# A written order for the mLSTM row factors, the attention splits and silu(z) in a hybrid decoder layer

## The chip, the cores and the metric

The kernel runs on one core of a Trainium2 chip. The metric is the device time of one launch in microseconds; for the kernel before it is the median of three runs. A fourth launch was taken by the profiler, and all rows below come from that one execution.

## The reference

One decoder layer on a sequence of 256 tokens and a width of 1024, all in float32: a half-step SwiGLU feed-forward block, a mixer, a second half-step feed-forward block, each with an RMS norm whose output is scaled and shifted by a vector made from the condition `c`, and a final RMS norm. The mixer is the part at hand:

```python
proj = h @ w_in                                  # q, k, v of attention, x_m, z
o_a = rmsnorm(attention(q_a, k_a, v_a), attn_norm)
x_conv = silu(causal_depthwise_conv(x_m))
h_m = mlstm(q_m, k_m, v_m, gates)                # num / max(|den|, exp(-m)) per row
h_m = (h_m - mean) * rsqrt(var + EPS) * mlstm_norm
o_m = (h_m + mlstm_skip * x_conv) * silu(z)
return concatenate([o_a, o_m]) @ w_out
```

With 256 tokens the attention has one block, so that it is plain causal attention of eight heads; the mLSTM has four heads of width 128.

## The kernel before

Data lie transposed: 128 features on the partitions, the 256 tokens along the free axis. Every weight is float32 and is split into a high and a low part (`whi` by a ScalarE copy, `wlo` by a VectorE subtraction, in pieces of 128x1024), every activation likewise (`hh`, `hl`; `hilo`, line 342), and a product is three matmuls (`mm3`, line 232): high by high, low by high, high by low. TensorE does little but these. Weights come in chunks of up to 1 MB through SP's DMA queue; a chunk gives two pieces, and five pieces of each kind fit, so a piece can be split as soon as the piece five places ahead of it has been multiplied (`weights`, line 219).

The order of the instructions on each engine is partly written, partly planned. The kernel hands its instructions to a planner, which lays each engine's instructions out by when it takes them to be ready. An instruction issued through `act`, `dve`, `pool` or `pe` while that engine's `on` flag is set is pinned: it stands behind the instruction issued just before it on the same engine in the program, whether or not that one was pinned itself. An unpinned one (the weight splits among them) can be put into any gap ahead of a pinned one that isn't ready. All loads on SP are pinned. The table load that ScalarE needs before a silu is put in after planning.

The stretch that is touched is the end of the mixer (lines 974 to 1011). In the program's order: the last attention pieces and `a_out` (pinned); the rest of the mLSTM sums; the third of four passes over the z columns (`next(g)`, each pass 24 matmuls, whose result goes through `shifted` into `zs`); `m_factors`, which makes one factor per token and head from the row sums (square, max, add, Ln, Exp, three VectorE operations of `newton`, and `spread`, which splits the result into `rows`); `z_silu(0)`, the silu of the first half of z; the fourth z pass; `z_silu(1)`; `m_out_pre` per head; and `hilo` of the attention tiles 1 to 3 into `hh[:, 1..3]` and `hl[:, 1..3]`. The output projection follows: its eight steps k (24 matmuls each) take the attention tiles (k = 0 to 3) and then the mLSTM tiles (k = 4 to 7). Tile 0 has a place of its own (`mix0`), split early. After step k = 2, `m_spread` lays the row factors over 128 partitions by four matmuls on `rows`; then `m_out` makes the mLSTM tiles. TensorE's order is pinned from line 974 to the end of step k = 3; ScalarE's and VectorE's is not pinned from line 981 on, but for the two `z_silu`, which are always pinned. The factor `mlstm_skip` is multiplied into `xc` by four ScalarE copies (line 986), and silu of z by four GpSimd products (line 822).

Of the kernel before, what the change touches and what calls it, by code (L numbers as in the profile page):

```python
# [13 lines left out]
AF = mybir.ActivationFunctionType  # L14
ALU = mybir.AluOpType
# [3 lines left out]
T = 256  # L19
# [4 lines left out]
NH = 4  # L24
# [12 lines left out]
C_SK = 128  # L37
# [23 lines left out]
def layer(ctx: ExitStack, tc: tile.TileContext, i, out: bass.AP):  # L61
# [511 lines left out]
    with tc.tile_pool(name="mix", bufs=1) as mp:  # L573
        mixer(tc, nc, i, mp, locals())
# [13 lines left out]
def mixer(tc, nc, i, mp, L):  # L588
    act, dve, pool, pe, sp = L["act"], L["dve"], L["pool"], L["pe"], L["sp"]
    nm, bank, t256, as32, dma = L["nm"], L["bank"], L["t256"], L["as32"], L["dma"]  # L590
    weights, part, mm3, hilo = L["weights"], L["part"], L["mm3"], L["hilo"]
    sm, hh, hl, tmp, eps_t = L["sm"], L["hh"], L["hl"], L["tmp"], L["eps_t"]
# [5 lines left out]
    def mt(shape, name, dt=F32, tag=None, bufs=1):  # L598
        return mp.tile(shape, dt, name=nm(name), tag=tag or name, bufs=bufs)

    def tiles(*done):

        w = weights()
        for g in range(2):
            pb = bank("b")
            for d in range(8):
                mm3(pb[:, 0:W], w, (g * 8 + d) * P, hh[:, d], hl[:, d], start=(d == 0), stop=(d == 7))
            done[g](pb)
            yield

    def shifted(dst):

        def done(pb):
            col = tmp.tile([P, 1], F32, tag="col", name=nm("col"), bufs=3)
            act.activation(col, pb[:, T:T + 1], AF.Copy)
            t = t256("ht", bufs=3)
            dve.tensor_tensor(t, r, pb[:, 0:T], ALU.mult)
            act.activation(dst, t, AF.Identity, bias=col)
        return done
# [42 lines left out]
    xc = mt([P, NH, T], "xc")  # L662
# [37 lines left out]
    def spread(src):  # L700

        act.activation(rows[0:4], src, AF.Copy)
        dve.tensor_tensor(rows[32:36], src, as32(rows[0:4]), ALU.subtract)
# [84 lines left out]
    def m_vars(h):  # L788
        pe.matmul(st["prow"][0:4, T:2 * T], ohc[:, h], st["sq", h], start=False, stop=(h == NH - 1),
                  skip_group_check=True)  # L790

    def m_factors():


        prow, em = st["prow"], st["em"]
        dd = mt([NH, T], "dd", tag="R2")
        act.activation(dd, prow[0:4, 0:T], AF.Square, scale=EPS ** 0.5)
        dve.tensor_tensor(dd, dd, em, ALU.max)
        vv = mt([NH, T], "vv", tag="R3")
        dve.scalar_tensor_tensor(vv, prow[0:4, T:2 * T], 1.0 / P, dd, ALU.mult, ALU.add)  # L800
        rs = mt([NH, T], "rs", tag="R1")
        act.activation(rs, vv, AF.Ln)
        act.activation(rs, rs, AF.Exp, scale=-0.5)
        newton(rs, vv, [NH, T], "r", 0.0)
        spread(rs)
# [4 lines left out]
    def mix(k):  # L810
        return mix0 if k == 0 else (hh[:, k, 0:T], hl[:, k, 0:T])

    zs = mt([P, NH, T], "zs")

    def z_silu(h2):
        z2 = zs[:, 2 * h2:2 * h2 + 2]
        tc.keep_in_program_order(act.activation(z2, z2, AF.Silu))

    def m_out_pre(h):

        dve.scalar_tensor_tensor(cn[:, h], cn[:, h], sm[:, C_MN + h:C_MN + h + 1], zs[:, h], ALU.mult, ALU.mult)
        pool.tensor_tensor(xc[:, h], xc[:, h], zs[:, h], ALU.mult)

    def m_spread():
        st["pb"] = [bank("b") for _ in range(2)]
# [13 lines left out]
    oa = mt([P, 4, T + 3], "oa", tag="A")  # L839
# [142 lines left out]
    m_sums(3)  # L982
    m_vars(1)
    m_vars(2)
    for h in range(NH):
        act.activation(xc[:, h], xc[:, h], AF.Copy, scale=sm[:, C_SK + h:C_SK + h + 1])
    g = tiles(shifted(zs[:, 2]), shifted(zs[:, 3]))
    side(1)
    next(g)
    m_vars(3)  # L990
    m_factors()
    z_silu(0)
    next(g)
    z_silu(1)
    for h in range(NH):
        m_out_pre(h)
    for j in range(1, 4):
        hilo(*mix(j), oa[:, j, 0:T])
    po = [bank(t) for t in ("m", "m", "a", "a")]
    for c in range(4):  # L1000
        w = weights()
# [100 lines left out]
```

## Time and profile before

| what | value |
|---|---|
| median of three runs | 534.91 us (534.86 to 535.97) |
| profiled execution, its own time | 537.05 us |
| its span, first to last instruction | 535.2 us |
| TensorE matmul busy | 517.4 us, 97% |
| VectorE busy | 423.4 us, 79% |
| ScalarE busy | 281.0 us, 53% |
| GpSimd busy | 46.9 us, 9% |
| mean granted TensorE clock | 0.989 |

An engine's busy time is the sum of its recorded instructions; shares are of the span. The granted clock is given as a share of the full one, 1.00 for 2.4 GHz and 0.50 for 1.2 GHz.

### The profile page before, as it was taken

What the parts mean: (1) busy time and instruction counts of PE and PEld (TensorE: products, weight loads), DVE (VectorE), ACT (ScalarE), POOL (GpSimd) and SP (SyncE); (2) the same over time, 40 slices, a digit from 0 to 9 for tenths busy, and PEclk for the clock granted to TensorE, in tenths of its full rate; (3) what the DMA queues carried; (4) which work ended last, traced back from release to release, by engine and by line L of the source; (5) the groups of instructions that cost most, each with busy time, mean ns of one, the idle gap of its engine ahead of it and who ended that gap; (6) DMA issues with size and microseconds to landing.
All of it is one profiled execution on the core that took longest, in us unless ns stands there. A gap on an engine that the chain in (4) does not pass through costs nothing.

```text
span 535.2 us, 9560 instructions
## 1 busy us (share of the span) xinstructions
PE 517.4 (97%) x3804; PEld 485.3 (91%) x3804; DVE 423.4 (79%) x714; ACT 281.0 (53%) x486; POOL 46.9 (9%) x64
## 2 busy tenths in 40 slices
PE   7999999899999999999999989999999999999992
PEld 7899999899988889988987889999999999988881
DVE  7898879999889997898885686989986776655423
ACT  4464436355555544566767554865545455544410
POOL 5000000000001110110000020400000000022220
PEclk9999999899999999999999999999999999999998
DMA  8997977988778998578631024488955455455002
GB/s 311 356 411 298 381 282 294 349 351 325 300 286 329 328 344 303 172 287 319 225 146 59 15 105 141 184 326 293 312 195 186 163 196 193 157 206 188 1 1 78
DMA packets 23951, 125.73 MB, mean 235 GB/s; under 512 B 2657, under 2 KB 2913, under 8 KB 14434
## 3 DMA queue, kind: packets, MB, share of 16 engines
q1 hardware_dynamic: 23618, 124.59, 62.2%
q8 instruction: 30, 0.49, 0.4%
q10 hardware_dynamic: 288, 0.52, 0.3%
q14 instruction: 15, 0.12, 0.1%
HBM read 124.05 MB, written 1.05 MB: 234 GB/s over the span
## 4 chain that ended last, share of the span: by engine, by line
PE 89%; DVE 4%; DMA 3%; issue 2%; ACT 1%; SPq 0%; DVEq 0%; ACTq 0%
PE psa L54 42%; PE psb L54 27%; PE psm L54 21%; DMA ada<-in_ada 2%; DMA x<-in_x 1%; DVE junk L54 1%; DVE wlo L54 1%; ACT whi L54 0%; DVE cn L54 0%; DVE u_out L54 0%; ACT sq L54 0%; DVE nw L54 0%; DVE half L54 0%; ACT zs L54 0%; DVE x L54 0%
## 5 line engine op out<-in xcount | busy, mean ns | idle before, releaser
L54 ACT ACTIVATE whi<-raw 128x1024 fp32r<-128x1024 f32 (+1 forms) x160 | 167.2, 1047 | 137.8 <-PE psa L54 62.4
L54 DVE TENSOR_TENSOR wlo<-raw,whi 128x1024 fp32r<-128x1024 f32 (+1 forms) x160 | 193.3, 1211 | 53.2 <-ACT whi L54 51.8
L54 PE MATMUL psa<-hh,whi 128*128 128x258 f32 (+1 forms) x388 | 110.1, 286 | 0.6 <-DVE gm L54 0.6
L54 PE MATMUL psa<-hh,wlo 128*128 128x258 f32 (+1 forms) x388 | 110.3, 286 | 0.0
L54 PE MATMUL psa<-hl,whi 128*128 128x258 f32 (+1 forms) x388 | 108.8, 285 | 0.0
L54 PE MATMUL psb<-hh,whi 128*128 128x258 f32 (+1 forms) x316 | 91.3, 290 | 2.3 <-ACT hh L54 1.2
L54 DVE SCALAR_TENSOR_TENSOR junk<-ada,c_bc 128x1024 bf16<-128x1024 f32 x72 | 88.1, 1224 | 3.4 <-DMA ada<-in_ada 3.3
L54 PE MATMUL psb<-hh,wlo 128*128 128x258 f32 (+1 forms) x316 | 89.4, 284 | 0.0
L54 PE MATMUL psb<-hl,whi 128*128 128x258 f32 (+1 forms) x316 | 88.9, 283 | 0.0
L54 PEld LDWEIGHTS psa<-hh,whi 128*128 128x128 f32 x388 | 74.4, 192 | 0.8 <-DVE gm L54 0.8
L54 PEld LDWEIGHTS psa<-hh,wlo 128*128 128x128 f32 x388 | 74.4, 192 | 0.1
L54 PEld LDWEIGHTS psa<-hl,whi 128*128 128x128 f32 x388 | 73.9, 192 | 0.0
L54 PEld LDWEIGHTS psb<-hh,whi 128*128 128x128 f32 x316 | 59.8, 189 | 5.3 <-issue 1.4
L54 PEld LDWEIGHTS psb<-hh,wlo 128*128 128x128 f32 x316 | 59.7, 189 | 0.1
L54 PEld LDWEIGHTS psb<-hl,whi 128*128 128x128 f32 x316 | 59.7, 190 | 0.0
L54 PE MATMUL psa<-g,whi 128*128 128x512 f32 x176 | 59.4, 395 | 0.0
L54 PE MATMUL psm<-hh,wlo 128*128 128x256 f32 (+1 forms) x200 | 56.9, 285 | 0.0
L54 PE MATMUL psm<-hh,whi 128*128 128x256 f32 (+1 forms) x200 | 56.8, 284 | 0.0
L54 PE MATMUL psm<-hl,whi 128*128 128x256 f32 (+1 forms) x200 | 56.6, 285 | 0.0
L54 PE MATMUL psa<-g,wlo 128*128 128x256 f32 x176 | 45.5, 281 | 0.0
L54 PEld LDWEIGHTS psa<-g,whi 128*128 128x128 f32 x176 | 32.5, 188 | 7.2
L54 PEld LDWEIGHTS psm<-hh,whi 128*128 128x128 f32 x200 | 38.2, 191 | 0.2
(241 smaller groups left out, 768.3 us busy)
## 6 DMA issues: line engine op xcount, KB each, us to landing
ada<-in_ada SPq DMA_DIRECT2D x72, 512.0 KB, 6.0
raw<-in_dn SPq DMA_DIRECT2D x22, 1024.0 KB, 4.8
raw<-in_guB SPq DMA_DIRECT2D x19, 1024.0 KB, 4.8
raw<-in_gu SPq DMA_DIRECT2D x18, 1024.0 KB, 7.1
raw<-in_gu SPq DMA_DIRECT2D x8, 512.0 KB, 7.6
raw<-in_wqk SPq DMA_DIRECT2D x4, 1024.0 KB, 5.8
raw<-in_wout SPq DMA_DIRECT2D x4, 1024.0 KB, 4.8
raw<-in_guA SPq DMA_DIRECT2D x4, 768.0 KB, 4.5
```

The lines of the kernel that those rows point to most:

```text
L54: r = f(*a, **k)
```

## The change

In `m_factors` the order of ScalarE and VectorE becomes pinned, and it stays so until behind `m_out_pre`. Within that stretch the `hilo` of the attention tiles 1 to 3 moves from behind `m_out_pre` to behind the fourth z pass, ahead of `z_silu(1)`. The four ScalarE copies that scale `xc` go away, and GpSimd's four products become VectorE operations that multiply by the skip factor and by silu of z at once.

```diff
     def m_factors():
         prow, em = st["prow"], st["em"]
+        act.on = dve.on = True
         dd = mt([NH, T], "dd", tag="R2")
...
     def m_out_pre(h):
         dve.scalar_tensor_tensor(cn[:, h], cn[:, h], sm[:, C_MN + h:C_MN + h + 1], zs[:, h], ALU.mult, ALU.mult)
-        pool.tensor_tensor(xc[:, h], xc[:, h], zs[:, h], ALU.mult)
+        dve.scalar_tensor_tensor(xc[:, h], xc[:, h], sm[:, C_SK + h:C_SK + h + 1], zs[:, h], ALU.mult, ALU.mult)
...
     m_vars(2)
-    for h in range(NH):
-        act.activation(xc[:, h], xc[:, h], AF.Copy, scale=sm[:, C_SK + h:C_SK + h + 1])
     g = tiles(shifted(zs[:, 2]), shifted(zs[:, 3]))
     side(1)
     next(g)
     m_vars(3)
     m_factors()
     z_silu(0)
     next(g)
+    for j in range(1, 4):
+        hilo(*mix(j), oa[:, j, 0:T])
     z_silu(1)
     for h in range(NH):
         m_out_pre(h)
-    for j in range(1, 4):
-        hilo(*mix(j), oa[:, j, 0:T])
+    act.on = dve.on = False
     po = [bank(t) for t in ("m", "m", "a", "a")]
```

## Rows read from the trace of the kernel before

**Rows 1.** Waits of TensorE between 285 and 345 us: total, times, longest.

```profile
PE psb L54 <- DVE rows L54: 1.6, 1, 1.6
```

**Rows 2.** The chain that ended last, 303 to 320 us: start, length, what.

```profile
304.05 2.98 PE psb L54 x23
...
316.26 0.90 DVE rows L54
```

**Rows 3.** Timeline of TensorE, 306 to 323 us: start, length, instruction, idle before.

```profile
306.85 0.28 PE L54 MATMUL psb<-hl,whi 128*128 128x258 f32 x1
306.98 0.28 PE L54 MATMUL psm<-mix0h,whi 128*128 128x256 f32 x1
...
309.85 0.29 PE L54 MATMUL psm<-hh,whi 128*128 128x256 f32 x1
...
312.71 0.28 PE L54 MATMUL psm<-hh,whi 128*128 128x256 f32 x1
...
317.30 0.70 PE L54 MATMUL psb<-rows,ohr 36*128 36x256 f32 x4 [1.57 <-DVE rows L54]
...
322.41 0.28 PE L54 MATMUL psm<-hh,whi 128*128 128x256 f32 x1
```

**Rows 4.** Busy time by stretch: us, PE, PEld, DVE, ACT, POOL, PEclk, DMA.

```profile
317.50:318.50 1.00, 1.00 (x8) 0.87 (x8) 1.00 (x3) 0.00 (x0) 0.24 (x1) 1.00 0.45 184
318.50:321.50 3.00, 3.00 (x17) 3.00 (x16) 3.00 (x8) 0.42 (x1) 0.00 (x0) 0.50 0.02 6
```

**Rows 5.** Timeline of TensorE, 95 to 104 us.

```profile
98.31 0.39 PE L54 MATMUL psb<-hh,whi 128*128 128x256 f32 x1 [1.15 <-ACT whi L54]
99.28 0.39 PE L54 MATMUL psa<-hh,whi 128*128 128x256 f32 x1 [0.58 <-DVE gm L54]
```

**Rows 6.** Busy time by stretch, 100 to 103 us.

```profile
100.00:103.00 3.00, 3.00 (x17) 3.00 (x16) 3.00 (x6) 0.00 (x0) 0.00 (x0) 0.51 0.95 356
```

**Rows 7.** Timeline of ScalarE, 303 to 321 us.

```profile
303.62 1.05 ACT L54 ACTIVATE whi<-raw 128x1024 fp32r<-128x1024 f32 x1
304.57 0.36 ACT L54 ACTIVATE dd<-psa 4x256 f32<-4x256 f32 x1
304.83 0.49 ACT L54 ACTIVATE zs<-ht,col 128x256 f32<-128x256 f32 x1
305.24 1.01 ACT L54 ACTIVATE hh<-oa 128x256 fp32r<-128x256 f32 x3
...
307.32 1.05 ACT L54 ACTIVATE whi<-raw 128x1024 fp32r<-128x1024 f32 x1
...
309.39 1.28 ACT L54 ACT_TABLE_LOAD   x1
310.69 0.63 ACT L54 ACTIVATE zs<-zs 128x512 f32<-128x512 f32 x1
311.22 1.04 ACT L54 ACTIVATE whi<-raw 128x1024 fp32r<-128x1024 f32 x1
...
320.92 0.42 ACT L54 ACTIVATE hh<-ht 128x256 fp32r<-128x256 f32 x1 [3.90 <-DVE ht L54]
```

**Rows 8.** Timeline of VectorE, 296 to 306 us.

```profile
296.32 0.42 DVE L54 SCALAR_TENSOR_TENSOR nw<-rr 128x256 f32<-128x256 f32 x1 [6.36 <-ACT rr L54]
296.78 0.42 DVE L54 SCALAR_TENSOR_TENSOR nw<-psa,nw 128x256 f32<-128x256 f32 x1
...
304.71 1.23 DVE L54 TENSOR_TENSOR wlo<-raw,whi 128x1024 fp32r<-128x1024 f32 x1 [0.53 <-ACT whi L54]
305.85 0.41 DVE L54 TENSOR_TENSOR dd<-dd,em 4x256 f32<-4x256 f32 x1
```

**Rows 9.** Instructions on the tile xc: ns min/median/max, first and last start.

```profile
L54 ACT ACTIVATE xc<-xc,sm x4: 507/517/557, 282.7 to 289.7; 128x256 f32<-128x256 f32 x4
L54 POOL TENSOR_TENSOR xc<-xc,zs x4: 730/824/922, 311.4 to 316.8; 128x256 f32<-128x256 f32 x4
```

**Rows 10.** Groups of instructions, 300 to 318 us: busy us, mean ns.

```profile
L54 DVE SCALAR_TENSOR_TENSOR cn<-cn,sm,zs 128x256 f32<-128x256 f32 x4 | 3.2, 834 | 1.4 <-ACT zs L54 1.4
L54 DVE SCALAR_TENSOR_TENSOR oa<-oa,sm,rr 128x256 f32<-128x256 f32 x3 | 1.3, 480 | 0.0
```

## The prediction

> **What bounds the kernel now.** I read four views in this order: who TensorE waits for, the chain that ended last, the engines' timelines around the place, the granted clock by stretch. TensorE is the bound: between 285 and 345 us, the stretch around the change, the view of waits has one line, 1.6 us for the `rows` of the row factors [rows 1], and the chain of waits leaves TensorE when the last z pass ends and comes back to it over `rows` [rows 2]. The reader is to see in the timeline that the passes and steps around it run without a gap, 2.87 us each (306.98 to 309.85 to 312.71), and that the wait of 1.57 us stands before `m_spread`, behind step k = 2 [rows 3]. The wait has a second price. About 1 us after TensorE starts again the granted clock falls to 0.50 for a little over 3 us, against 1.00 before [rows 4]. The trace has a second such place: idle times of 1.15 and 0.58 us just after each other at 98 to 99 us [rows 5], and behind them a stretch at 0.51 [rows 6]. Three us at half the clock do the work of 1.5 us, so the price of the low stretch is 1.5 us. What the change can win at most is thus 1.57 + 1.5 = 3.07 us: if `rows` came in time and nothing else were late.
>
> **What goes.** In the pinned order neither a `cn` nor the silu of the second half of z stands ahead of `rows` any more, and GpSimd no longer runs beside VectorE. The bare chain below has `rows` at about 309.8, with the splits that may get in at 312.5, and TensorE wants it at 312.71 + 2.87 = 315.6 [rows 3]. So the wait before `m_spread` goes with its low stretch: 1.57 + 1.5 = 3.07 us.
>
> **What comes.** The written order also pins the splits of the attention tiles behind the row factors and behind `z_silu(0)`. Before, the planner put these three ScalarE copies at 305.24, over a microsecond before their first reader was due; step k = 1 needs `hh[:, 1]` at 309.85 [rows 3, 7]. Now ScalarE has to do, in this order: `zs` of the third pass, `dd`, Ln, Exp, the copy of `rows`, the table load, `z_silu(0)`, the column and `zs` of the fourth pass, and only then `hh[:, 1]`. The waiting instruction is the copy of `rows`, which waits for VectorE's three `newton` operations; behind it stand all the others, and TensorE waits for them, its order being pinned as well. The splits issue three copies on ScalarE and three subtractions on VectorE and no DMA; SP's queue sees nothing but later room for weights.
>
> The bare chain, step by step:
> - `whi` starts at 303.62 and holds ScalarE for 0.95 us until 304.57; then `zs`, 0.41 to the next start (304.83 to 305.24), then `dd` at 304.98, done by 305.3 [rows 7].
> - On VectorE `wlo` is ahead, and `dd` goes on at 305.85 as before [rows 8]. `vv` follows at the spacing of two operations that depend on each other, 0.46 us (296.32 to 296.78) [rows 8]: 306.31. I take the same 0.46 for each hand-over that follows: Ln 306.77, Exp 307.23, `newton` 307.69, 308.15 and 308.61, the copy of `rows` 309.07.
> - The copy holds ScalarE for about 0.3 us, by the spacing of the other operation on 4 partitions, 0.26 (304.57 to 304.83) [rows 7]: 309.35. Table load 1.28 and silu 0.53 (310.69 to 311.22) [rows 7]: 311.2. The column, about 0.1, and `zs`, 0.41: 311.7. The copy into `hh[:, 1]`, a third of 1.01 us with its tail, 0.4 [rows 7]: done at 312.1.
>
> TensorE would then wait from 309.85 to 312.1, that is 2.25 us. That is the lower end of the wait.
>
> The upper end comes from the unpinned weight splits, which the planner puts wherever a pinned instruction isn't ready. A `whi` becomes possible when the last z pass ends (about 307.1) [rows 3], just about when Exp is due (307.23), and ran at 307.32 before; the next one becomes possible at 309.85, when step k = 0 is done, and ran at 311.22 before [rows 3, 7]. Both fall into the new chain, the second either before the copy of `rows` or between the column and `zs`, since the planner doesn't count the table load (put in afterwards) and so sees a gap there. Each holds ScalarE for 0.95 us. If both delay the chain: 2.25 + 2 x 0.95 = 4.15 us. If one does: 3.2 us, and then its `wlo`, 1.14 us to the next start (304.71 to 305.85) [rows 8], stands before the subtraction into `hl[:, 1]`, which the third matmul of step k = 1 needs; up to 0.6 us more. I take 3.9 us, between these two, because each of the two `whi` becomes ready within 0.5 us of the pinned instruction that it would pass.
>
> A wait of that size brings the low clock too, as both cases in the trace did: another 1.5 us [rows 4 to 6]. The bounds are 0 (one of two is no law) and 3.0 (two such stretches).
>
> **What costs nothing.** The four copies that leave ScalarE, 4 x 0.517 = 2.07 us between 282.7 and 289.7 [rows 9], stood where TensorE waits for nobody [rows 1]: 0. On VectorE four products come in. The trace has no such operation on `xc`; the nearest of the same form without GpSimd beside it took 0.480 us, the one beside GpSimd 0.834 [rows 10]. I take 0.48, since GpSimd's four products of 0.824 go away [rows 9]: 4 x 0.48 = 1.9 us come, 4 x (0.834 - 0.480) = 1.4 us go, so +0.5 us with bounds of 0 and +1.9. The eight operations run while TensorE is in steps k = 1 and k = 2; without that cover they would delay `m_out` by 8 x 0.48 = 3.8 us.
>
> What is late next: the first mLSTM tile. It came at 320.92 + 0.42, 4.0 us after the start of `m_spread`, and step k = 4 started 5.1 us after it, at 322.41 [rows 3, 7], because step k = 3 ran at the low clock. At full clock step k = 4 comes 0.7 + 2.87 = 3.6 us after the start of `m_spread`. A new wait of up to 0.4 us is possible there; GpSimd's products no longer stand before it, so I take 0.
>
> **The sum.** 3.9 + 1.5 - 3.07 = +2.3 us. The profiled execution, 535.2 us of span and 1.85 us around it, took 537.05 us; it would become 539.4. It lies 2.1 us above the median of the runs, and the sum rests on differences inside one execution, so I set it on the median: 534.91 + 2.3 = 537.2 us.
>
> ScalarE's table load is where the skill and the trace differ. Here the silu starts at 310.69, 0.02 us behind the 1.28 us of the load [rows 7]. The Trainium skill (ScalarE: Activation LUTs, What ACT_TABLE_LOAD costs) counts a drain of about 1.38 us beside the load, some 2.66 us for a switch. By that the sum would be 1.4 us larger, 538.6 us; by the trace it stays at 537.2, and the trace decides.
>
> **The rivals.**
> - Faster: the splits come in time. Mechanism: the chain on ScalarE and VectorE to `hh[:, 1]` is at least 2.25 us shorter than I make it, and the point that decides is 309.85, the end of step k = 0. Price: 0 there and 3.07 won, 531.8 us. Half of it, an idle time of 1.1 us without the low clock (if `dd` passes the `wlo` of 1.14 us in front of it), gives 1.1 - 3.07 = -2.0, 532.9 us. For it: the chain was lengthened by splits in the gaps before. Against it: seven dependent hand-overs, a table load and a silu lie on it, and `dd` starts no earlier than the third z pass lets it.
> - The bare chain: both `whi` fall outside it. 2.25 + 1.5 - 3.07 = +0.7, 535.6 us, within 0.2% (1.07 us, about what a measurement can tell from no change). For it: Ln is due 0.3 us before the first `whi` becomes possible. Against it: in the trace a `whi` stands at both moments.
> - A second wait: step k = 4 or a second low stretch. +2.3 + 0.4 to 1.5 us, 537.6 to 538.7 us; with both splits on the chain, 539. For it: the cover of `m_out` gets thinner by the clock. Against it: VectorE has its eight products done by then. The longer table load that the page gives would land here as well, and the trace speaks against it.
> - Nothing moves: the planner's order was this one already. The trace excludes it for the splits (305.24) and the silu (310.69) [rows 7]; 534.9 us.
>
> **How the numbers follow.** The forecast, one or two splits on the chain (3.2 to 4.4 us, so 536.4 to 537.9 us): 0.57. Faster: 0.14. Bare chain: 0.14, of which 0.03 lie above 0.2%. A second wait: 0.12, of which 0.02 for the page's table load. Nothing: 0.03. Slower by over 0.2% is 0.57 + 0.12 + 0.03 = 0.72, within 0.2% is 0.11 + 0.03 = 0.14, faster is 0.14. The range of 8 in 10 leaves out most of the faster case and the end of the second wait: 533.8 to 538.9 us.
>
> **What would show it.** In the profile of the changed kernel TensorE waits before step k = 1 for ScalarE's `hh` (or VectorE's `hl`), 2 to 4.5 us, and no longer for `rows`; ScalarE shows `rows`, table load, silu, `zs`, `hh` in this order, with `whi` among them; a stretch at 0.50 follows in steps k = 1 and 2; `cn` takes 0.48 us. I am wrong if TensorE reaches step k = 1 and finds `hh` there, or if the low stretch stays away.

## The result, and the profile after

| | before | after |
|---|---|---|
| median of 8 runs, us | 535.98 (534.86 to 537.16) | 539.46 (538.42 to 540.73) |
| ratio to before | | 1.0067 (1.005 to 1.0085) |
| profiled execution, span, us | 535.2 | 536.8 |
| first matmul of step k = 0, us | 306.98 | 304.76 |
| first residual behind the output projection, us | 331.89 | 333.48 |
| between these two, us | 24.91 | 28.72 |

The change makes the kernel slower by 0.67%, 3.6 us. One execution of e1 below ran at a granted clock of 0.56, took 845 us and is left out of its ratio.

The two spans differ by less, 1.6 us, because the execution of before lost more time ahead of the change. At 28 us TensorE waits 1.2 us for an `hh` there and not at all in that of after; at the two idle times of [rows 5] after is 1.0 us ahead. And these two idle times, which after has as well, 1.15 and 0.59 us, brought the low stretch of [rows 6] in before and none in after (timeline of TensorE and busy time by stretch, after):

```profile
97.34 0.39 PE L54 MATMUL psb<-hh,whi 128*128 128x256 f32 x1 [1.15 <-ACT whi L54]
98.31 0.39 PE L54 MATMUL psa<-hh,whi 128*128 128x256 f32 x1 [0.59 <-DVE gm L54]
```

```profile
100.00:103.00 3.00, 3.00 (x28) 3.00 (x27) 3.00 (x7) 0.83 (x2) 0.00 (x0) 1.00 1.01 381
```

When step k = 0 starts, after is 2.2 us ahead. So I compare from the first matmul of step k = 0 to the first residual behind the output projection, which these differences don't reach; there the change costs 3.81 us, within the interval of the ratio (2.7 to 4.6 us). The next rows are the residuals, first of before, then of after (timeline of VectorE).

```profile
331.89 0.88 DVE L54 SCALAR_TENSOR_TENSOR x<-psm,gt,x 128x256 f32<-128x256 f32 x2 [1.20 <-PE psm L54]
```

```profile
333.48 0.88 DVE L54 SCALAR_TENSOR_TENSOR x<-psm,gt,x 128x256 f32<-128x256 f32 x2 [1.25 <-PE psm L54]
```

Who TensorE waits for between 285 and 345 us, after. The wait for `rows` [rows 1] is gone, and a wait for `hh` three times as long has come.

```profile
PE psm L54 <- ACT hh L54: 4.8, 1, 4.8
```

The timeline of TensorE after: step k = 0 starts at 304.76, its last matmul at 307.52, and step k = 1 at 312.56 [rows 3].

```profile
304.76 0.28 PE L54 MATMUL psm<-mix0h,whi 128*128 128x256 f32 x1
...
307.52 0.28 PE L54 MATMUL psa<-mix0l,whi 128*128 128x256 f32 x1
312.56 0.58 PE L54 MATMUL psm<-hh,whi 128*128 128x256 f32 x1 [4.76 <-ACT hh L54]
...
317.35 0.28 PE L54 MATMUL psm<-hh,whi 128*128 128x256 f32 x1
```

The timeline of ScalarE after is the written chain, with what got into it: two small copies (`hh<-sh`) and a `whi` ahead of Ln, a second `whi` ahead of `rows` [rows 7].

```profile
302.76 0.36 ACT L54 ACTIVATE dd<-psa 4x256 f32<-4x256 f32 x1
304.84 0.32 ACT L54 ACTIVATE hh<-sh 128x8 fp32r<-128x8 f32 x2 [1.72 <-PE psb L54]
305.06 1.04 ACT L54 ACTIVATE whi<-raw 128x1024 fp32r<-128x1024 f32 x1
306.01 0.40 ACT L54 ACTIVATE rs<-vv 4x256 f32<-4x256 f32 x1
306.44 0.42 ACT L54 ACTIVATE rs<-rs 4x256 f32<-4x256 f32 x1
307.84 1.06 ACT L54 ACTIVATE whi<-raw 128x1024 fp32r<-128x1024 f32 x1 [0.98 <-PE psa L54]
308.80 0.40 ACT L54 ACTIVATE rows<-rs 4x256 fp32r<-4x256 f32 x1
309.22 1.28 ACT L54 ACT_TABLE_LOAD   x1
310.51 0.63 ACT L54 ACTIVATE zs<-zs 128x512 f32<-128x512 f32 x1
311.05 0.15 ACT L54 ACTIVATE col<-psb 128x1 f32<-128x1 f32 x1
311.69 0.51 ACT L54 ACTIVATE zs<-ht,col 128x256 f32<-128x256 f32 x1 [0.49 <-DVE ht L54]
312.10 1.02 ACT L54 ACTIVATE hh<-oa 128x256 fp32r<-128x256 f32 x3
```

VectorE after: the second half of each split stands in the chain as well, one ahead of `newton`, one ahead of `rows`; and `ht`, with VectorE idle for 0.63 us, waits for ScalarE's `col` [rows 8].

```profile
306.13 1.23 DVE L54 TENSOR_TENSOR wlo<-raw,whi 128x1024 fp32r<-128x1024 f32 x1 [0.54 <-ACT whi L54]
307.28 0.41 DVE L54 SCALAR_TENSOR_TENSOR nw<-rs 4x256 f32<-4x256 f32 x1
...
308.93 1.23 DVE L54 TENSOR_TENSOR wlo<-raw,whi 128x1024 fp32r<-128x1024 f32 x1 [0.35 <-ACT whi L54]
310.18 0.42 DVE L54 TENSOR_TENSOR rows<-rs,rows 4x256 fp32r<-4x256 f32 x1
311.23 0.42 DVE L54 TENSOR_TENSOR ht<-rr,psb 128x256 f32<-128x256 f32 x1 [0.63 <-ACT col L54]
```

Busy time by stretch after: the clock falls while TensorE still waits, and stays at 0.50 until step k = 1 is nearly done; before, it fell only behind the wait [rows 4].

```profile
309.50:312.50 3.00, 0.00 (x0) 0.00 (x0) 1.49 (x3) 2.50 (x6) 0.00 (x0) 0.55 0.42 127
312.50:316.50 4.00, 3.94 (x18) 3.95 (x19) 3.96 (x11) 1.14 (x4) 0.00 (x0) 0.50 0.24 101
317.00:320.00 3.00, 3.00 (x28) 3.00 (x27) 1.23 (x1) 1.06 (x1) 0.00 (x0) 1.00 0.03 5
```

### The profile page after: what moved, and what is told of

Same layout as the page of the kernel before. It is cut to its first block, busy times and chain, and to the rows that moved or that the text cites. A ratio compares the mean times of both kernels' runs of the same rounds, so it can differ in the third digit from the quotient of the medians.

```text
span 536.8 us, 9552 instructions
## 1 busy us (share of the span) xinstructions
PE 517.5 (96%) x3804; PEld 484.9 (90%) x3804; DVE 423.9 (79%) x718; ACT 280.2 (52%) x482; POOL 42.5 (8%) x60
## 4 chain that ended last, share of the span: by engine, by line
PE 93%; DVE 3%; ACT 2%; DMA 1%; issue 1%; SPq 0%; DVEq 0%; ACTq 0%
PE psa L54 43%; PE psb L54 27%; PE psm L54 22%; DMA x<-in_x 1%; DVE junk L54 1%; ACT whi L54 0%; DVE u_out L54 0%; DVE wlo L54 0%; DVE nw L54 0%; ACT sq L54 0%; ACT L54 0%; DVE half L54 0%; ACT zs L54 0%; DVE x L54 0%; DVE rr L54 0%
```

## The experiments

The theory: the loss is the new place of the splits, behind row factors, table load and silu. The rivals: the pinned order of the row factors or the products on VectorE cost it; the chain is long by itself and not by the weight splits; the clock has another cause. Each kernel was timed in five rounds against the kernel before; beside the ratio stands the stretch from step k = 0 to the first residual, from one profile each (24.91 us before, 28.72 us after).

| kernel | ratio (95% interval) | stretch, us | waits of TensorE in it, us | low clock in it |
|---|---|---|---|---|
| e1, splits ahead of the row factors | 1.0004 (0.9988 to 1.002) | 24.14 | 1.45 and 0.30 | none |
| e2, products alone | 1.0006 (0.9993 to 1.002) | 24.77 | 0.82 and 1.45 | none |
| e3, wait filled | 1.0054 (1.0039 to 1.0069) | 27.18 | 0.49 | none |
| e4, weight splits behind | 1.0046 (1.003 to 1.0062) | 27.08 | 3.25 | yes |
| e5, no table load | 1.0048 (1.0031 to 1.0065) | 28.00 | 4.15 | yes |
| e6, order alone | 1.0056 (1.0035 to 1.0077) | 28.40 | 4.76 | yes |
| e7, mLSTM tiles in pairs | 0.9959 (0.9944 to 0.9974) | 22.45 | none | none |

**e1: the splits ahead of the row factors.** The edit against the changed kernel:

```diff
     m_vars(3)
+    next(g)
+    for j in range(1, 4):
+        hilo(*mix(j), oa[:, j, 0:T])
     m_factors()
     z_silu(0)
-    next(g)
-    for j in range(1, 4):
-        hilo(*mix(j), oa[:, j, 0:T])
     z_silu(1)
```

> The fourth z pass and the splits of the attention tiles are issued ahead of the row factors, all else as in the changed kernel. Theory (the splits stand behind table load and silu): TensorE finds hh at step k = 1, no wait of 4.76 us and no low clock there; rows come at about 312.5 against 315.6 wanted, so no wait before m_spread either. 3.07 us below the kernel before, ratio 0.994; up to 1.3 us of that may go to a wait of step k = 4 for the first mLSTM tile (0.997). Rival (the pinned order of the row factors or the products on VectorE cost the time, wherever the splits stand): ratio stays at 1.004 to 1.007.

The whole loss is gone, with the row factors pinned and the products on VectorE as in the changed kernel: the place of the splits is the cause. (Issued ahead of `m_factors`, they are also no longer pinned; place and pin go together here.) But hardly anything was won. `rows` comes in time, and then TensorE waits for the next thing, the first mLSTM tile of step k = 4 (timeline of TensorE):

```profile
319.56 0.38 PE L54 MATMUL psm<-hh,whi 128*128 128x256 f32 x1 [1.45 <-ACT hh L54]
321.07 0.39 PE L54 MATMUL psm<-hl,whi 128*128 128x256 f32 x1 [0.30 <-DVE hl L54]
```

That tile (`ht`) is late because two unpinned `wlo` stand on VectorE, one ahead of its two operations and one between them (timeline of VectorE):

```profile
315.20 1.21 DVE L54 TENSOR_TENSOR wlo<-raw,whi 128x1024 fp32r<-128x1024 f32 x1
316.33 1.07 DVE L54 TENSOR_TENSOR ht<-cn,psb 128x256 f32<-128x256 f32 x3
317.32 1.21 DVE L54 TENSOR_TENSOR wlo<-raw,whi 128x1024 fp32r<-128x1024 f32 x1
318.46 1.08 DVE L54 TENSOR_TENSOR ht<-ht,xc 128x256 f32<-128x256 f32 x3
```

The ratio lies above the 0.994 to 0.997 expected. In the one profile the stretch is 0.77 us shorter than before, 0.14%, which is just outside the ratio's interval; by the ratio nothing was won.

**e2: the products alone.** The edit against the kernel before:

```diff
-        pool.tensor_tensor(xc[:, h], xc[:, h], zs[:, h], ALU.mult)
+        dve.scalar_tensor_tensor(xc[:, h], xc[:, h], sm[:, C_SK + h:C_SK + h + 1], zs[:, h], ALU.mult, ALU.mult)
...
-    for h in range(NH):
-        act.activation(xc[:, h], xc[:, h], AF.Copy, scale=sm[:, C_SK + h:C_SK + h + 1])
```

> The kernel before with the products alone changed (one VectorE operation per head, no ScalarE copies, no GpSimd), nothing pinned. Theory (the products are not the loss): VectorE is done with cn and xc some 0.35 us earlier and rows takes 0.42 instead of 0.89 us, so the wait before m_spread shrinks from 1.57 to about 0.7 us; 0.8 us below the kernel before if the low clock stays, 2.3 us if it goes: ratio 0.9955 to 0.9985. Rival (four more operations on VectorE cost time): the wait grows by up to 1.9 us, ratio 1.001 to 1.0035.

The wait for `rows` shrank as expected, from 1.57 to 0.82 us, and no low clock followed. The time did not fall, and the ratio lies above the 0.9955 to 0.9985 expected: the first mLSTM tile is late here too, by the same 1.45 us. In before the low stretch in step k = 3 had covered it (waits of TensorE, 300 to 345 us):

```profile
PE psm L54 <- ACT hh L54: 1.5, 1, 1.5
PE psb L54 <- DVE rows L54: 0.8, 1, 0.8
```

**e3: the wait filled with matmuls of no use.** The edit against the changed kernel:

```diff
+                if (k, d) == (0, 7):
+                    pf = bank("a")
+                    for _ in range(36):
+                        pe.matmul(pf[:, 0:T], L["ones_r"], mix0[0], start=True, stop=True)
```

> The changed kernel with 36 matmuls of no use issued behind step k = 0, so that TensorE is busy for 4.3 of the 4.76 us in which it waits for hh. Theory (the wait brings a low clock, a price of its own of 1.9 us): step k = 1 starts when it did, no stretch at 0.50 behind it, 1.9 us below the changed kernel, ratio to before 1.003. Rival (the low clock comes from elsewhere or its price is hidden): the stretch stays, ratio 1.0067 as in the changed kernel.

`hh` comes as late as before the filling (0.49 us of wait are left behind 4.43 us of filling), but the granted clock stays at 1.00 throughout. A low stretch starts within the wait or behind it in all four profiles that have a wait of 3.25 us or more there, and here there is none: it goes with the wait. It was worth 1.54 us of the stretch, 28.72 to 27.18, where I expected 1.9. The 1.9 took step k = 1 at 2.87 us; behind a wait it takes 3.24 us even at full clock, as the starts of steps k = 1 and k = 2 show. The ratio, expected at 1.003, fell only from 1.0067 to 1.0054; the intervals overlap, so that the gain rests on the two profiles. Timeline of TensorE, and busy time by stretch, filled wait and what follows:

```profile
313.98 0.39 PE L54 MATMUL psm<-hh,whi 128*128 128x256 f32 x1 [0.49 <-ACT hh L54]
...
317.22 0.28 PE L54 MATMUL psm<-hh,whi 128*128 128x256 f32 x1
```

```profile
309.00:313.90 4.90, 4.49 (x38) 4.28 (x37) 2.99 (x6) 4.13 (x8) 0.00 (x0) 1.00 0.23 73
314.00:317.00 3.00, 3.00 (x23) 2.84 (x24) 3.00 (x9) 1.07 (x3) 0.00 (x0) 1.00 0.33 135
```

**e4: the weight splits behind the second silu.** The edit against the changed kernel; `issue_after` places what ScalarE issues inside it behind the named instruction:

```diff
-    z_silu(1)
+    last = z_silu(1)
...
-        w = weights()
+        with tc.issue_after(last.ins) if c == 1 else ExitStack():
+            w = weights()
```

> The changed kernel with the two weight splits that got into the chain put behind the second silu. Theory as forecast (each whi on the chain costs 0.95 us): the wait falls from 4.76 to about 3 us, 1.5 to 1.9 us below the changed kernel, ratio 1.003 to 1.004. Rival (the chain is that long without them: the table load, the column that VectorE waits for, the hand-overs): wait 4.2 us or more, ratio 1.0055 to 1.0067.

The wait falls by 1.5 us to 3.25 us, where about 3 was expected, and the ratio to 1.0046, where 1.003 to 1.004 was: the two splits cost 1.5 us, not 1.9, and without them the chain is 1 us longer than the 2.25 us I had worked out. The timeline of ScalarE shows where: Ln stands behind the two small copies, which wait 1.71 us for the last z pass, and `zs` behind `ht`, which VectorE did not start before `col` was done.

```profile
303.67 0.36 ACT L54 ACTIVATE dd<-psa 4x256 f32<-4x256 f32 x1
305.74 0.32 ACT L54 ACTIVATE hh<-sh 128x8 fp32r<-128x8 f32 x2 [1.71 <-PE psb L54]
305.95 0.40 ACT L54 ACTIVATE rs<-vv 4x256 f32<-4x256 f32 x1
...
311.07 0.51 ACT L54 ACTIVATE zs<-ht,col 128x256 f32<-128x256 f32 x1 [0.49 <-DVE ht L54]
```

**e5: no table load.** The edit against the changed kernel, which leaves the silu of z out: `AF.Silu` becomes `AF.Copy` in `z_silu`.

> The changed kernel without silu of z (a copy in its place), so that ScalarE needs no table load at this point; nothing else moves. Theory (the load lies on the chain with its whole length): the wait before step k = 1 falls by 1.3 us, from 4.76 to about 3.5 us; 1.3 us below the changed kernel, ratio to before 1.004. If a drain of another 1.4 us came with the load: 2.7 us, wait 2.1 us, ratio 1.0015. Rival (the load is covered by the matmuls of step k = 0): no change, ratio 1.0067.

The wait fell by 0.6 us, not by 1.3. Without the load ScalarE is ready for the last `zs` at 310.7, but its input `ht` isn't there: it stands on VectorE behind `rows`, and that behind the second `wlo`. Two ways lead to `hh`, nearly equally long, and taking 1.28 us from one uncovers the other after 0.6 us (timeline of VectorE):

```profile
309.88 1.22 DVE L54 TENSOR_TENSOR wlo<-raw,whi 128x1024 fp32r<-128x1024 f32 x1 [0.35 <-ACT whi L54]
311.13 0.41 DVE L54 TENSOR_TENSOR rows<-rs,rows 4x256 fp32r<-4x256 f32 x1
311.58 0.42 DVE L54 TENSOR_TENSOR ht<-rr,psb 128x256 f32<-128x256 f32 x1
```

**e6: the written order alone.** The edit against the changed kernel is that of e2 taken back.

> The changed kernel with the products as before (four ScalarE copies, four GpSimd products). Theory (the written order is the whole loss, the products none): the wait before step k = 1 is 4.5 to 5 us as in the changed kernel, GpSimd's products lie behind it; ratio 1.006 to 1.008. Rival (the products carry part of the loss): wait under 4.3 us, ratio 1.002 to 1.005.

The wait is the same 4.76 us, and the stretch 3.49 us longer than before, against 3.81 with the products. The whole difference, 0.32 us, lies in step k = 1, 4.47 us here and 4.79 in after, and is the clock's: here it fell at 312.2, 4.7 us after the wait began, and was back at 315.6; in after it was back at 316.6, with step k = 1 starting at 312.31 here and at 312.56 there. So the order is the loss, and the products cost nothing that these profiles show. The ratio, 1.0056, lies a little under the 1.006 to 1.008 expected. Timeline of TensorE, starts of steps k = 1 and k = 2:

```profile
312.31 0.58 PE L54 MATMUL psm<-hh,whi 128*128 128x256 f32 x1 [4.76 <-ACT hh L54]
...
316.78 0.28 PE L54 MATMUL psm<-hh,whi 128*128 128x256 f32 x1
```

On VectorE, `cn` takes 0.717 us on the mean with GpSimd's products running and 0.480 without (groups by line, of this kernel and of after):

```profile
L54 DVE SCALAR_TENSOR_TENSOR cn<-cn,sm,zs 128x256 f32<-128x256 f32 x4 | 2.6, 717 | 0.0
```

```profile
L54 DVE SCALAR_TENSOR_TENSOR cn<-cn,sm,zs 128x256 f32<-128x256 f32 x4 | 1.9, 480 | 0.0
```

**e7: the mLSTM tiles in pairs.** From e1, `m_spread` moves to the middle of step k = 2, `m_out` makes two tiles at a time in pinned order (its new body is not shown), and the weight splits of the last chunks stand behind the first pair:

```diff
-                if (k, d) == (2, 7):
+                if (k, d) == (2, 3):
                     m_spread()
-                    for h in range(NH):
+                    act.on = dve.on = True
+                    for h in (0, 2):
                         m_out(h)
+                    act.on = dve.on = False
...
-        w = weights()
+        with tc.issue_after(st["tile", 1].ins) if c > 1 else ExitStack():
+            w = weights()
```

> The kernel with the splits issued ahead of the row factors, and further: m_spread stands in the middle of step k = 2, the mLSTM tiles are made two at a time in pinned order, and the weight splits of the last chunks stand behind the first pair. Theory (what was left of the gain went into the first mLSTM tile, 1.45 and 0.30 us of wait before and in step k = 4): that tile comes at about 316.8 on the clock of the first run of this line, 1 us before it is wanted; no wait from the third z pass on; from the first matmul of step k = 0 to the first residual 22 to 22.4 us, against 24.9 before and 24.1 without the pairs; 2.5 us below the kernel before, ratio 0.995. Rival (TensorE's own order and speed bound this stretch): stays at 24 us, ratio 1.000.

This one beats both kernels: 534.18 us against 536.67 us of the kernel before on the same chip, ratio 0.9959 where 0.995 was expected, stretch 22.45 us where 22 to 22.4 was. The first pair's `hh` starts at 317.59, step k = 4 finds it there, and TensorE doesn't wait in the whole stretch. Which of the edits behind e1 gave how much was not separated. Busy time, 304 to 330 us:

```profile
304.00:314.00 10.00, 10.00 (x84) 10.00 (x84) 8.31 (x18) 8.65 (x19) 0.00 (x0) 1.00 0.32 94
314.00:330.00 16.00, 16.00 (x133) 15.73 (x132) 13.18 (x27) 6.82 (x11) 0.00 (x0) 1.00 0.46 157
```

## Why the prediction was right and wrong

**The direction and the place were right.** The wait before `m_spread` went; a wait for `hh[:, 1]` came before step k = 1, because the splits had been pinned behind the silu; a low stretch followed. e1, e3 and e6 bear this out.

**The time was outside the range.** I had 537.2 us and at most 538.9; it is 539.46 us. Of the 2.3 us between, 1.07 us are the base: the sum was set on a median of three launches, 534.91 us, and over all eight it is 535.98. The rest is the loss itself, +2.3 us in the sum, +3.6 us by the ratio and +3.81 us in the stretch. There 4.93 us more go by from step k = 0 to step k = 1 (4.76 of them the wait) and 1.92 us more in step k = 1 (4.79 against 2.87); 1.63 us less go by ahead of `m_spread` and 1.47 us less in step k = 3. So what was to go went, 3.10 us against 3.07 forecast, and the new low stretch cost 1.55 us (4.79 against 3.24 in e3) against 1.5. Missing in the sum are above all 0.86 us of the wait, 4.76 against 3.9, and 0.37 us by which step k = 1 is slower behind a wait even at full clock. (A slip beside it: waits of 3.2 to 4.4 us give 536.5 to 537.7 us by the sum, not 536.4 to 537.9.)

**The step that failed is the bare chain, "2.25 us ... the lower end of the wait".** It measures 3.25 us (e4). Two things were missing. The planner put two small copies, `hh<-sh`, into the gap between `dd` and Ln; they overwrite columns of `hh` that the last z pass still reads, so ScalarE, which takes its instructions in order, stood for 1.71 us, and Ln came about 0.5 us late. The prediction doesn't name these copies; it had nothing but weight splits in the gaps. And it let `ht` run beside the column; in the rows here `ht` starts only when ScalarE's `col` is done, which puts about 0.5 us more on the chain. `ht` doesn't read `col`; why it waits, no run shows. The splits, "2 x 0.95" at most and 1.65 taken, cost 1.5 us: close, but by luck. The first `whi` holds ScalarE ahead of Ln for 0.95 us, its `wlo` delays `newton` by about 0.4 us more, and the second `whi` costs only about 0.2 us, because it mostly fills a gap in which ScalarE waits for VectorE.

**The low clock was right, for a reason that was half chance.** The prediction rests it on two places in the trace. The second one, behind 1.15 and 0.58 us of idle time at 98 us, is no rule: the same two idle times stand in all nine profiles, and a stretch at 0.50 follows them in three (before, e3, e7) and in none of the other six.

**The old wait and its low stretch went, but going alone they win nothing.** "What the change can win at most is thus 1.57 + 1.5 = 3.07 us: if `rows` came in time and nothing else were late." Something was: in e1 and e2 the first mLSTM tile kept TensorE for 1.45 us. I had looked at that tile, found up to 0.4 us, and taken 0; it was late by 1.45 us, in e1 because two weight splits stand ahead of it on VectorE. In the changed kernel it is covered by the long wait itself, so it doesn't enter the result, but the case "faster" was priced too well by it: even with the splits in time, e1, the kernel is level with before.

**The products were priced right.** Eight operations at 0.480 us each, hidden; the forecast had 0.48. The Trainium skill (SBUF — State Buffer, Who interferes with whom) says that a VectorE instruction with two inputs from SBUF contends with a GpSimd instruction that reads SBUF; the rows of e6 agree in kind, 0.717 us with those products running against 0.480 without.

**The table load was priced right, but not its effect.** It took 1.28 us and the silu started 0.01 us behind it (309.22, 310.51). The Trainium skill (ScalarE: Activation LUTs, What ACT_TABLE_LOAD costs) counts a drain of about 1.38 us beside the load; it doesn't show here either. On the chain the load was worth only 0.6 us (e5).

## What to carry to other kernels

A written order is a promise about every instruction in it: whatever is issued behind a chain of dependent steps becomes as late as the chain, even if its data have long been there; so issue what the bound engine needs next ahead of the chain, as e1 does. And unpinned work still gets into the gaps of a pinned chain, with its own waits. Before a wait is counted as a gain, look for the next thing that would be late without it, and for what the low clock behind it covers: the gain came only in e7, where the splits and the tile both came in time. And compare one profile with another over the stretch that an edit touches: the whole span also holds waits and low stretches that come and go by themselves.

## What the runs showed of the hardware

In these profiles a low clock of TensorE came only with idle time of it. In the stretch around the change, single waits of 1.57, 3.25, 4.15 and (twice) 4.76 us were accompanied by a stretch at 0.50 (1.2 GHz); waits of 1.45 us, with another of 0.30 or 0.82 us some microseconds apart, were not, in one profile each; and with the longest wait filled by matmuls of no use the clock stayed at 1.00. The size of the idle time alone doesn't settle it. The pair of 1.15 and 0.58 us at 98 us was followed by a stretch at 0.50 in three of nine profiles and not in six. And of the two waits of 4.76 us, one had the clock fall 2.0 us after it began (after) and one only after 4.7 us (e6); in after it came back 4.1 us after TensorE started again, in e6 3.3 us. The same kernel's executions differ by up to 2.3 us (534.86 to 537.16 us); where two profiles can be laid side by side, the difference ahead of the change came from a wait at 28 us and from the low stretch at 100 us. A change of half a per cent is read better from the stretch that it touches than from two spans.
